# Queries' squares and query-key products as a step of their own, and eight modulation chunks in layer 0's output product instead of beside the recurrence

## The chip, the cores and the metric

The kernel runs on one core of a Trainium2 chip. The metric is the device time of one execution in microseconds (us). Five engines work side by side, each through its own queue in order: TensorE (PE, matrix products, with a separate row PEld for its weight loads), VectorE (DVE), ScalarE (ACT), GpSimd (POOL) and SyncE (SP), which only issues DMAs. Before the change the median of three runs is 1326.55 us (1324.47 to 1327.31).

## The reference

The model has two layers over 512 latent tokens of width 1024, with 256 context tokens beside them. Layer 0 mixes tokens by a bidirectional gated DeltaNet with four heads and, beside it, by pooling; layer 1 by convolutions. Each mixer is followed by a normalisation, and then by a convolutional feed-forward network (FFN) and a second normalisation. Cut to what this case touches:

```
for layer in range(2):
    mod = silu(c) @ ada_w[layer] + ada_b[layer]         # shift, scale, gate of both halves of a layer
    u = x * (1 + sc_m) + sh_m
    y = even_mixer(u, ctx_u, ...) if layer == 0 else odd_mixer(u, ...)
    x = layernorm(ALPHA * x + gt_m * y)
    y = conv_ffn(x * (1 + sc_f) + sh_f)
    x = layernorm(ALPHA * x + gt_f * y)

even_mixer:  p = u @ w_in                               # q, k, v, gate, pool, scalars
    q, k, v = silu(dwconv(p[...])); q, k = l2norm(q), l2norm(k)
    per head and chunk: a_mat = (k beta) k^T * decay;  solve (a_mat + 1);  attn = (q k^T) * decay
    recurrence over chunks, forward and backward:  v_new = u - w s;  o = q s + attn v_new;  s = s g + k v_new
    y = concat(norm(o) * silu(gate), pool(p)) @ w_out
```

The modulation vector for everything behind the first normalisation inputs is 80 columns of 128 numbers; one "chunk" below is one of these columns.

## The kernel before, in words

A product in fp32 is done as three products of split operands: a weight tile `w_raw` is rounded by ACT into `w_hi` (L167), its rest `w_lo` is formed by POOL or DVE (L173), and TensorE does `w_hi` with the high part of the activations (`ah`), `w_hi` with the low part (`al`), and `w_lo` with `ah` (the function `gemm`, L219).

Layer 0's mixer (`even`) runs a written plan, the string PLAN, one step after the other in program order. Heads are handled in two pairs, p0 and p1. In it k, q and v are the keys, queries and values of a pair (input product named `qkv_ps`, taps of a convolution on DVE, silu on ACT), e forms the systems of a pair, i and x the inverses, r the recurrence, p and w the pooling of one channel group, g a gate, d the normalised output. The system step makes decay factors (POOL forms `r` at L864, TensorE sums them into `dd_ps` at L866, ACT takes the exponential), the key-key products `kk_ps` (L885), and a small inverse whose 16x16 blocks go through a scratch buffer in memory twice (ACT issues those DMAs: L926, L930, L945, L948). The query step forms the queries; in the same step, ACT squares them (`q_sq`, L1022), TensorE sums the squares (`qn_ps`, L1025) and multiplies keys with queries (`kq_ps`, L1031), and DVE multiplies the products with the decay factors (L1034). The sums are read only by the output step, the products only by the recurrence.

Program order is not the order in which an engine works: a scheduler of the tile framework picks, for each engine, the order of its queue from the order of the program and its own estimates. On the chip each queue then runs strictly in that order.

The modulation chunks (`ada_rest`) are spread over the layer. One chunk is two DMAs of 256 KB (L360, queue of SP) and two DVE instructions of 128x512 that multiply and sum (L362), each followed by a short read of the accumulator. Before the change twelve chunks are done within step x0 (AX0 = 12) and eight within step r1 (AX1 = 8), so that twenty are done when the plan ends (`a20`). The last four before the first normalisation are done in layer 0's output product (`run`, `between`), one after each of the first four of eight output tiles (ADE = 1), from a pool of six buffers. That pool, with the tiles of the residual (`z`), comes after the mixer's pools and takes their memory.

Of the kernel before, what the change touches and what calls it, by code (L numbers as in the profile page):

```python
# [8 lines left out]
F32 = mybir.dt.float32  # L9
# [5 lines left out]
P = 128  # L15
T = 512
# [24 lines left out]
)  # L41
EVEN_SHAPES = (("tri", (4, P)), ("par", (3, P)), ("lvl", (2, P)), ("blk", (P,)), ("rev", (P,)), ("poolw", (4, P)),
               ("id16", (16,)), ("up16", (16,)), ("low16", (16,)))
PLAN = 'b0 k0 k1 e0 q0 n0 e1 q1 v0 g0 i0 n1 v1 g1 x0 p0 p1 r1 p2 g2 w2 p3 w0 g3 w3 d0 w1 d1 a20'
NI = 3
NX = 4
SHARE = 0.4
# [3 lines left out]
SHARE_DOWN = 0.5  # L51
LAST = (4, 4)
LAST_FFN = 2
ADE = 1
LATE2 = 3
READY = (2, 2)
FIRST = (3, 3, 3)
# [7 lines left out]
RINGS = ("001", "1")  # L65
RINGS_ODD = ("01", "1")
RINGS_ADA = ("01", "1")
AX0 = 12
AX1 = 8
R2 = 1  # L70
SHARE_EVEN = 0.1
# [30 lines left out]
def together(chains, n, each=None):  # L102

    active = []
    while chains or active:
        while chains and len(active) < n:
            active.append(chains.pop(0))
        for x in list(active):
            if next(x, 0) == 0:
                active.remove(x)  # L110
        if each:
            each()


class Kernel:
# [512 lines left out]
    def even(self):  # L628
        nc, a = self.nc, self.a
        with ExitStack() as ctx:  # L630
            self.rings = EVEN_RINGS
            cp = self.pool("ctx", ctx=ctx)
            km = cp.tile([P, a["even_k"].shape[1]], F32, name="even_k")
            for name, (o, shape) in EVENS.items():
                v = km[:, o:o + math.prod(shape)]
                setattr(self, name, v if len(shape) == 1 else v.rearrange("p (a b) -> p a b", b=shape[1]))
            self.ep = self.pool("even", ctx=ctx)
            self.ada_tile = lambda k: self.ep.tile([P, T], F32, tag="ada", bufs=self.bufs["ada"], name="ada_w")
            first, scal = self.start(km)
            self.ep2 = self.pool("even2", ctx=ctx)  # L640
            self.dp = ctx.enter_context(self.tc.tile_pool(name="scratch", bufs=1, space=bass.MemoryType.DRAM))
            self.gate = [None] * H
            ps, pooled, self.decays = {}, [], {}
            left = [[AX0, AX1]]

            def each(i):
                def f():
                    if left[0][i] and self.ada_next < 24:
                        left[0][i] -= 1
                        self.ada_rest(1, True)  # L650
                return f

            steps = dict(
                k=lambda p: ps.__setitem__(p, self.keys(p, None if p else first)),
                b=lambda p: self.gates(scal),
                t=lambda p: self.decays.__setitem__(p, self.decay(p)),
                n=lambda p: self.norms([ps[0], ps[1]] if p == 2 else [ps[p]]),
                e=lambda p: self.systems(p, ps[p]),
                v=lambda p: self.values(p, ps[p]),
                q=lambda p: self.queries(p, ps[p]),  # L660
                i=lambda p: together(self.inverses(p, ps[p]), NI),
                r=lambda p: together(self.recurrence(p, ps[p]), 2, each(1)),
                x=lambda p: together(self.recurrence(0, ps[0]) + self.inverses(1, ps[1]), NX, each(0)),
                y=lambda p: together(self.inverses(0, ps[0]) + self.inverses(1, ps[1]), NX),
                z=lambda p: together(self.recurrence(0, ps[0]) + self.recurrence(1, ps[1]), 4),
                a=lambda n: self.ada_rest(n - self.ada_next, True),
                g=lambda h: self.gating(h),
                p=lambda g: pooled.append(self.pooling(g)),
                w=lambda g: self.pool_out(g, pooled[g]),
                d=lambda p: together(self.gdn_out(p, ps[p]), 4),  # L670
            )
            for w in PLAN.split():
                steps[w[0]](int(w[1:]))
            for i, x in enumerate([*pooled, *self.gate]):
                self.split(x, self.ah[i], self.al[i], nc.vector if i % 2 else None)
        self.dbg("mixh", self.ah)
        self.dbg("mixl", self.al)
# [335 lines left out]
    def queries(self, p, s):  # L1013
        nc = self.nc
        qx = s["q"] = (self.lat("ql", f"p{p}"), None)
        for i in range(2):
            self.qkv(2 * p + i, qx[0][i], None)
        qs = s["qs"] = self.small("qss", [4, 2])
        pn = self.gd("qn_ps")
        for h in range(2):  # L1020
            sq = self.big("q_sq")[:, 0:T]
            nc.scalar.activation(out=sq, in_=qx[0][h], func=AF.Square)  # L1022
            for i in range(4):
                o = 2 * (2 * i + h)
                nc.tensor.matmul(out=pn[:, o:o + 2], lhsT=sq[:, i * P:(i + 1) * P], rhs=self.ones[:, 0:2], start=True,  # L1025
                                 stop=True)
        for j in (1, 2):
            ps = self.gd4("kq_ps")
            for q in range(4):
                c = 2 * j + q // 2  # L1030
                nc.tensor.matmul(out=ps[:, q], lhsT=self.chunk(s["k"], c, q % 2), rhs=self.chunk(qx, c, q % 2),  # L1031
                                 start=True, stop=True)
            e = s["e"][j]
            nc.vector.tensor_tensor(out=e, in0=ps, in1=e, op=MUL)  # L1034

        nc.vector.tensor_scalar(out=qs, in0=pn[:, 0:16].rearrange("p (c h t) -> p c h t", h=2, t=2)[:, :, :, 0],
                                scalar1=RMS_EPS * P, scalar2=RMS_EPS * RMS_EPS * P, op0=MUL, op1=ADD)
# [262 lines left out]
    def run(self):  # L1300
        nc, a = self.nc, self.a
        self.share = SHARE_EVEN
        self.late = iter(())
        self.ready = []
        self.cols = {}
        self.constants()
        self.bufs = BUFS
        pa = self.pool("a")
        self.ah = [pa.tile([P, T], F32R, name=f"ah{k}") for k in range(KD)]
        self.al = [pa.tile([P, T], F32R, name=f"al{k}") for k in range(KD)]  # L1310
        self.wp = self.pool("w")
        self.ps = self.pool("ps", psum=True)
        self.turn = {}
        self.even()
        if self.stop == "even":
            return
        self.rings = RINGS
        up = self.pool("u")
        self.uh = [up.tile([P, T], F32R, name=f"uh{k}") for k in range(KD)]
        self.ul = [up.tile([P, T], F32R, name=f"ul{k}") for k in range(KD)]  # L1320
        self.tp = self.pool("tmp")
        zp = self.pool("z")
        self.zs = [zp.tile([P, T], F32, name=f"z{k}") for k in range(KD)]
        for k in range(KD):
            nc.sync.dma_start(out=self.zs[k], in_=a["xT"][:, k])
            nc.scalar.activation(out=self.zs[k], in_=self.zs[k], func=AF.Copy, scale=ALPHA)
        self.gt_m0 = self.mods(0, 8, "mod_g")
        with ExitStack() as ctx:
            ap = self.pool("ada", ctx=ctx)
            self.ada_tile = lambda k: ap.tile([P, T], F32, tag="ada", bufs=6, name="ada_w")  # L1330
            def between(m):
                if self.ada_next < 24:
                    self.ada_rest(min(ADE, 24 - self.ada_next))
                    if self.ada_next >= 24:
                        self.columns(0)

            ring = lambda nm: ap.tile([P, T], F32R, tag="w", bufs=4 * LAST[0], name=nm)
            self.out_proj(a["even_out"], KD, self.ah, self.al, self.gt_m0, 0, self.uh, self.ul,
                          ahead=AHEAD, ring=ring, between=between,
                          first=[a["ffn_up"][0, i * KF] for i in range(READY[0])])  # L1340
        self.dbg("xm0", self.zs)
        if self.stop == "mix0":
            return

        self.ffn(0, lambda: self.gt_f0, 1)
        self.dbg("xf0", self.zs)
        if self.stop == "ffn0":
            return
        self.odd()
        self.dbg("xm1", self.zs)  # L1350
        if self.stop == "mix1":
            return
        self.ffn(1, lambda: self.gt_f1, None)
# [91 lines left out]
```

## Time and profile before

| | us |
|---|---|
| median of three runs | 1326.55 |
| lowest and highest | 1324.47, 1327.31 |
| the profiled execution's own time | 1322.59 |
| its span, first to last instruction | 1320.8 |

| engine | busy us | share of the span | instructions |
|---|---|---|---|
| PE | 1259.7 | 95% | 6690 |
| DVE | 912.2 | 69% | 1874 |
| POOL | 669.1 | 51% | 607 |
| ACT | 583.0 | 44% | 1091 |

The mean granted clock of TensorE is 0.985. These shares are means over stages: layer 0's mixer takes about the first 330 us, the output product of layer 0 runs from there to about 403 us, and behind that come FFN 0, layer 1 and FFN 1. In the FFNs TensorE is busy nearly all the time; in the mixer DVE and TensorE take turns at waiting. The busy rows show how full an engine was in a stretch; the waits, which engine and instruction it was that ended an idle time.

### The profile page before, as it was taken

How to read it: one execution, taken by the hardware profiler on the slowest of the kernel's cores; microseconds unless marked ns; L12 is line 12 of the kernel's file. 1: busy time of each engine (PE TensorE's matmuls, PEld its weight loads, DVE VectorE, ACT ScalarE, POOL GpSimd, SP SyncE). 2: the span in 40 equal slices, each digit the busy share in tenths (PEclk: the TensorE clock that was granted, in tenths of full speed). 3: DMA queues.
4: the chain of work that ended last, by engine and by line, in shares of the span. 5: the costliest groups of instructions: out<-in, count | busy, mean ns of one | idle time of the engine just before them, and what ended most of it. 6: DMA issues, size and time to landing. Idle time of an engine off the chain costs nothing.

```text
span 1320.8 us, 19563 instructions
## 1 busy us (share of the span) xinstructions
PE 1259.7 (95%) x6690; PEld 1062.0 (80%) x6690; DVE 912.2 (69%) x1874; ACT 583.0 (44%) x1091; POOL 669.1 (51%) x607
## 2 busy tenths in 40 slices
PE   6998889988899999999999999899999999999997
PEld 3877778877798888888888887688988888888886
DVE  3778899998777877788444568857786666661125
ACT  3645324356556333333322684535653333332235
POOL 2354466665426555555344667954243443433453
PEclk9998899999999999999999999999999999999998
DMA  9511213431623656556565432233032233333334
GB/s 363 194 49 39 66 45 112 145 113 32 216 88 118 193 195 196 193 192 195 171 210 155 147 95 84 69 96 128 18 112 96 96 97 100 99 92 96 95 111 135
DMA packets 100340, 166.58 MB, mean 126 GB/s; under 512 B 20432, under 2 KB 25616, under 8 KB 100240
## 3 DMA queue, kind: packets, MB, share of 16 engines
q1 hardware_dynamic: 89280, 164.09, 38.9%
q10 hardware_dynamic: 10960, 1.25, 0.7%
q8 instruction: 53, 0.87, 0.3%
q14 instruction: 47, 0.39, 0.1%
HBM read 162.60 MB, written 2.69 MB: 125 GB/s over the span
## 4 chain that ended last, share of the span: by engine, by line
PE 62%; DVE 6%; ACT 3%; POOL 2%; issue 2%; DMA 1%; POOLq 0%; ACTq 0%; SPq 0%
PE prod_ps L219 36%; PE out_ps L219 21%; PE half_ps L219 2%; DVE conf_y L1236 2%; PE ln_e L417 1%; POOL w_lo L173 1%; POOL conf_far L1225 1%; DVE z L478 1%; PE ln_w L427 1%; DVE w_lo L173 1%; ACT w_hi L167 1%; DVE ln_d L424 1%; ACT ln_u L490 0%; DMA w_raw<-in_even_out 0%; DVE ln_s L404 0%
## 5 line engine op out<-in xcount | busy, mean ns | idle before, releaser
L173 POOL TENSOR_TENSOR w_lo<-w_raw,w_hi 128x512 fp32r<-128x512 f32 (+1 forms) x302 | 392.8, 1304 | 456.4 <-ACT w_hi L167 441.0
L167 ACT CAST w_hi<-w_raw 128x512 fp32r<-128x512 f32 (+1 forms) x408 | 245.7, 608 | 457.0 <-PE prod_ps L219 140.2
L219 PE MATMUL prod_ps<-uh,w_lo 128*128 128x512 f32 x792 | 309.8, 391 | 5.0 <-POOL w_lo L173 3.7
L219 PE MATMUL prod_ps<-uh,w_hi 128*128 128x512 f32 x792 | 309.3, 391 | 2.7 <-ACT w_hi L167 2.7
L219 PE MATMUL prod_ps<-ul,w_hi 128*128 128x512 f32 x792 | 309.2, 390 | 0.0
L604 DVE SCALAR_TENSOR_TENSOR f_acc<-prod_ps,prm,f_acc 128x441 f32<-128x441 f32 (+2 forms) x320 | 222.2, 694 | 61.4 <-ACT f_acc L593 52.1
L219 PEld LDWEIGHTS prod_ps<-uh,w_lo 128*128 128x128 f32 x792 | 149.4, 189 | 37.8 <-POOL w_lo L173 5.0
L219 PEld LDWEIGHTS prod_ps<-uh,w_hi 128*128 128x128 f32 x792 | 149.3, 189 | 33.7 <-ACT w_hi L167 3.1
L219 PEld LDWEIGHTS prod_ps<-ul,w_hi 128*128 128x128 f32 x792 | 149.3, 188 | 31.0
L173 DVE TENSOR_TENSOR w_lo<-w_raw,w_hi 128x512 fp32r<-128x512 f32 (+1 forms) x106 | 85.0, 802 | 123.5 <-ACT w_hi L167 121.6
L219 PE MATMUL out_ps<-ah,w_lo 128*128 128x256 f32 (+1 forms) x352 | 118.1, 335 | 3.8 <-DVE w_lo L173 3.8
L219 PE MATMUL out_ps<-ah,w_hi 128*128 128x256 f32 (+1 forms) x352 | 118.1, 336 | 1.6 <-ACT ah L456 1.6
L219 PE MATMUL out_ps<-al,w_hi 128*128 128x256 f32 (+1 forms) x352 | 118.7, 337 | 0.0
L219 PE MATMUL out_ps<-hh,w_lo 128*128 128x512 f32 (+1 forms) x280 | 99.2, 354 | 1.9 <-POOL w_lo L173 1.9
L219 PE MATMUL out_ps<-hh,w_hi 128*128 128x512 f32 (+1 forms) x280 | 98.7, 352 | 0.1
L219 PE MATMUL out_ps<-hl,w_hi 128*128 128x512 f32 (+1 forms) x280 | 98.6, 352 | 0.0
L362 DVE SCALAR_TENSOR_TENSOR ada_w<-ada_w,crow_ps 128x512 f32<-128x512 f32 x112 | 70.7, 682 | 10.1 <-DMA ada_w<-in_ada 10.1
L219 PEld LDWEIGHTS out_ps<-ah,w_lo 128*128 128x128 f32 x352 | 67.0, 190 | 10.8 <-DVE w_lo L173 4.1
L219 PEld LDWEIGHTS out_ps<-ah,w_hi 128*128 128x128 f32 x352 | 67.0, 191 | 8.7 <-ACT ah L456 2.0
L219 PEld LDWEIGHTS out_ps<-al,w_hi 128*128 128x128 f32 x352 | 67.2, 191 | 7.5 <-DVE al L457 0.8
L219 PEld LDWEIGHTS out_ps<-hh,w_lo 128*128 128x128 f32 x280 | 53.4, 191 | 9.7 <-POOL w_lo L173 2.1
L219 PEld LDWEIGHTS out_ps<-hh,w_hi 128*128 128x128 f32 x280 | 53.4, 191 | 7.9 <-ACT w_hi L167 0.3
(362 smaller groups left out, 2285.9 us busy)
## 6 DMA issues: line engine op xcount, KB each, us to landing
w_raw<-in_ffn_up SPq DMA_DIRECT2D x176, 256.0 KB, 2.6
ada_w<-in_ada SPq DMA_DIRECT2D x160, 256.0 KB, 3.7
w_raw<-in_ffn_down SPq DMA_DIRECT2D x100, 256.0 KB, 2.8
w_raw<-in_even_in SPq DMA_DIRECT2D x40, 256.0 KB, 2.8
w_raw<-in_odd_in SPq DMA_DIRECT2D x40, 256.0 KB, 2.9
ada_w<-in_ada SPq DMA_DIRECT2D x16, 512.0 KB, 8.4
w_raw<-in_even_out SPq DMA_DIRECT2D x16, 256.0 KB, 2.9
w_raw<-in_odd_out SPq DMA_DIRECT2D x16, 256.0 KB, 2.7
```

The costliest lines, as they stand in the source:

```text
L167: r = nc.scalar.copy(out=hi[:, :n], in_=raw)
L173: r = eng.tensor_tensor(out=lo[:, :n], in0=raw, in1=hi[:, :n].bitcast(F32), op=SUB)
L219: r = nc.tensor.matmul(out=o, lhsT=w, rhs=x[k][:, c0:c1], start=clear and k == i == 0, stop=k == n - 1 and i == 2, skip_group_check=pin)
L362: r = nc.vector.scalar_tensor_tensor(out=w, in0=w, scalar=1.0, in1=c, op0=MUL, op1=MUL, accum_out=self.mod[:, k, i:i + 1])
L417: nc.tensor.matmul(out=pe[:, 2 * (n * e + i):2 * (n * e + i) + 2], lhsT=t[:, i * P:(i + 1) * P], rhs=ones, start=e == 0 and i == 0 and not ...
L424: nc.vector.tensor_tensor(out=d[:, 0:n], in0=self.ident[:, None, :].broadcast_to([P, n, P]), in1=x.broadcast_to([P, n, P]), op=MUL)
L427: nc.tensor.matmul(out=o, lhsT=self.ones, rhs=d[:, 0:n].rearrange("p a b -> p (a b)"), start=True, stop=True)
L478: nc.vector.tensor_tensor(out=z, in0=z, in1=x, op=op)
L604: nc.vector.scalar_tensor_tensor(out=o, in0=sv[:, r0 + dr:r1 + dr, q0 + dc:q1 + dc], scalar=w[:, tap:tap + 1], in1=o, op0=MUL, op1=ADD)
L1225: nc.gpsimd.tensor_tensor(out=far, in0=far, in1=f, op=ADD)
L1236: nc.vector.scalar_tensor_tensor(out=o, in0=pa[:, max(0, d):T - max(0, -d)], scalar=w[:, tap:tap + 1], in1=o, op0=MUL, op1=ADD)
```

## The change

The query step is cut in two. Forming the queries stays where it was (q0, q1 in the plan); the squares, their sums and the key-query products become the step u, which stands in the plan behind the values of the same pair: u0 behind v0, u1 behind v1. Step x0 does eight modulation chunks and no longer twelve, sixteen are done when the plan ends, and layer 0's output product does two after each of the first four output tiles, eight in all, from a pool of eight buffers.

```diff
-PLAN = 'b0 k0 k1 e0 q0 n0 e1 q1 v0 g0 i0 n1 v1 g1 x0 p0 p1 r1 p2 g2 w2 p3 w0 g3 w3 d0 w1 d1 a20'
+PLAN = 'b0 k0 k1 e0 q0 n0 e1 q1 v0 u0 g0 i0 n1 v1 u1 g1 x0 p0 p1 r1 p2 g2 w2 p3 w0 g3 w3 d0 w1 d1 a16'
-ADE = 1
+ADE = 2
-AX0 = 12
+AX0 = 8
                 q=lambda p: self.queries(p, ps[p]),
+                u=lambda p: self.attention(p, ps[p]),
...
         for i in range(2):
             self.qkv(2 * p + i, qx[0][i], None)
+
+    def attention(self, p, s):
+
+        nc = self.nc
+        qx = s["q"]
         qs = s["qs"] = self.small("qss", [4, 2])
         pn = self.gd("qn_ps")
         for h in range(2):
...
-            self.ada_tile = lambda k: ap.tile([P, T], F32, tag="ada", bufs=6, name="ada_w")
+            self.ada_tile = lambda k: ap.tile([P, T], F32, tag="ada", bufs=8, name="ada_w")
             def between(m):
                 if self.ada_next < 24:
                     self.ada_rest(min(ADE, 24 - self.ada_next))
```

From the new method on, lines are six further down in the changed kernel (L1025 is L1031 there); between L659 and there they are one further down.

On TensorE, where the squares of the first pair are summed before (`qn_ps`), right behind the first of the queries' input products, and ahead of the second pair's decay sums (`dd_ps`) and key-key products (`kk_ps`):

```order
L219 MATMUL qkv_ps<-ah_74,w_hi 128x512
L219 MATMUL qkv_ps<-al_82,w_hi 128x512
L219 MATMUL qkv_ps<-ah_74,w_lo 128x512
L1025 MATMUL qn_ps<-ones,q_sq 128x2 x4
L1031 MATMUL kq_ps<-ql,kl 128x128 x3
L1025 MATMUL qn_ps<-ones,q_sq 128x2 x4
L1031 MATMUL kq_ps<-ql,kl 128x128 x5
L866 MATMUL dd_ps<-r,even_k 128x256 x12
L885 MATMUL kk_ps<-kc 128x128 x4
L885 MATMUL kk_ps<-kl 128x128 x8
```

The same sums and products in the changed kernel, 118 places further on, with input products on both sides:

```order
L219 MATMUL qkv_ps<-ch,w_lo 128x256
L219 MATMUL qkv_ps<-ch,w_hi 128x256
L219 MATMUL qkv_ps<-cl,w_hi 128x256
L1031 MATMUL qn_ps<-ones,q_sq 128x2 x4
L1037 MATMUL kq_ps<-ql,kl 128x128 x2
L1031 MATMUL qn_ps<-ones,q_sq 128x2 x4
L1037 MATMUL kq_ps<-ql,kl 128x128 x6
L992 MATMUL it_ps<-r_1507,kk 128x128 x2
```

The sums now stand in front of the first product of the inverses (`it_ps`). The second pair's decay sums have moved the other way: in the changed kernel they stand only twelve input products (the last three are shown) behind the first pair's key-key products, where 77 stood between before.

```order
L886 MATMUL kk_ps<-kc 128x128 x4
L886 MATMUL kk_ps<-kl 128x128 x8
L219 MATMUL qkv_ps<-al_89,w_hi 128x512
...
L219 MATMUL qkv_ps<-al_84,w_hi 128x512
L219 MATMUL qkv_ps<-ah_76,w_lo 128x512
L219 MATMUL qkv_ps<-ah_77,w_hi 128x512
L867 MATMUL dd_ps<-r,even_k 128x256 x12
L886 MATMUL kk_ps<-kc 128x128 x4
L886 MATMUL kk_ps<-kl 128x128 x8
```

On DVE, from the last low parts of the mixer's output (`al_89`) through the modulation chunks (`ada_w`) to the first `w_lo` of the output product, before:

```order
L457 TENSOR_TENSOR al_89<-gate,ah_81 128x512
L362 SCALAR_TENSOR_TENSOR ada_w,mod<-ada_w,crow 128x512
L524 SCALAR_TENSOR_TENSOR z_3479<-out_ps,mod_g,z_3479 128x512
L362 SCALAR_TENSOR_TENSOR ada_w,mod<-ada_w,crow 128x512 x3
L524 SCALAR_TENSOR_TENSOR z_3480<-out_ps,mod_g,z_3480 128x512
L362 SCALAR_TENSOR_TENSOR ada_w,mod<-ada_w,crow 128x512
...
L404 TENSOR_TENSOR ln_s_3622<-ln_s_3622,ln_sq 128x512
L362 SCALAR_TENSOR_TENSOR ada_w,mod<-ada_w,crow 128x512 x2
L173 TENSOR_TENSOR w_lo<-w_raw,w_hi 128x512
```

The end of the same stretch in the changed kernel, where nine further chunk instructions stand ahead of the rows shown:

```order
L362 SCALAR_TENSOR_TENSOR ada_w,mod<-ada_w,crow 128x512 x5
L524 SCALAR_TENSOR_TENSOR z_3458<-out_ps,mod_g,z_3458 128x512
L362 SCALAR_TENSOR_TENSOR ada_w,mod<-ada_w,crow 128x512
L401 TENSOR_TENSOR ln_s_3597<-ln_s_3597,z_3458 128x512
L404 TENSOR_TENSOR ln_s_3598<-ln_s_3598,ln_sq 128x512
L362 SCALAR_TENSOR_TENSOR ada_w,mod<-ada_w,crow 128x512
L173 TENSOR_TENSOR w_lo<-w_raw,w_hi 128x512
```

Between `al_89` and the first `w_lo` there were 8 chunk instructions, 3 of `z` and 4 of the normalisation's sums; now there are 16, 4 and 6. On SP the 16 chunk loads stand in one run ahead of the eight loads of `even_out`, where 8 stood before.

## Rows read from the trace of the kernel before

**Rows 1.** By stage: start:end, length, busy us (instructions) of each engine, clock, DMA, GB/s.

```profile
92.50:112.00 19.50, 15.56 (x82) 12.88 (x80) 17.39 (x33) 9.07 (x14) 15.68 (x22) 1.00 0.22 52
112.00:145.00 33.00, 33.00 (x173) 29.32 (x173) 29.52 (x77) 14.80 (x20) 12.13 (x13) 0.90 0.16 47
145.00:165.00 20.00, 15.96 (x89) 14.56 (x88) 16.41 (x35) 7.82 (x14) 8.64 (x10) 0.83 0.31 59
190.00:290.00 100.00, 93.04 (x635) 80.56 (x636) 93.27 (x252) 42.54 (x122) 68.71 (x80) 1.00 0.34 109
345.00:368.00 23.00, 18.86 (x122) 17.50 (x121) 21.05 (x39) 9.71 (x18) 8.66 (x6) 0.93 0.57 180
```

The engines stand in the order PE, PEld, DVE, ACT, POOL.

**Rows 2.** PE's waits, 40 to 420 us: who waited for whom, total us, times, longest.

```profile
PE qn_ps L1025 <- ACT q_sq L1022: 6.7, 2, 3.5
PE out_ps L219 <- DVE w_lo L173: 3.8, 1, 3.8
PE it_ps L991 <- DVE r L984: 3.7, 7, 1.0
```

**Rows 3.** ACT in time, at both stalls: start, duration, what, [idle before <- releaser].

```profile
105.29 0.41 ACTq L926 DMA_DIRECT2D scr<-cb  x1
...
109.06 0.35 ACTq L930 DMA_DIRECT2D a<-scr  x1
...
146.86 0.34 ACTq L930 DMA_DIRECT2D a<-scr  x1
```

**Rows 4.** PE in time, decay and key-key products of the first pair.

```profile
84.45 5.51 PE L866 MATMUL dd_ps<-r,even_k 128*128 128x256 f32 x22
...
90.69 1.95 PE L885 MATMUL kk_ps<-kl 128*128 128x128 f32 x16
```

**Rows 5.** POOL in time, decay factors of the second pair.

```profile
97.32 6.22 POOL L864 TENSOR_TENSOR r<-even_k,sc_g 128x256 f32<-128x256 f32 x10
```

**Rows 6.** DVE groups, 205 to 300 us: count, busy us, mean ns, idle before.

```profile
L362 DVE SCALAR_TENSOR_TENSOR ada_w<-ada_w,crow 128x512 f32<-128x512 f32 x40 | 36.4, 946 | 0.2 <-issue 0.2
```

**Rows 7.** PE in time, the last recurrence products and the gate products behind them.

```profile
317.11 0.61 PE L1112 MATMUL o_ps<-vn,at 128*128 128x128 f32 x4
...
320.10 0.39 PE L219 MATMUL gate_ps<-ah,w_lo 128*128 128x512 f32 x1
320.32 0.39 PE L219 MATMUL gate_ps<-ah,w_hi 128*128 128x512 f32 x1
```

**Rows 8.** POOL in time, the last two of four additions of pooling group 3.

```profile
312.30 2.42 POOL L1172 TENSOR_TENSOR pool_q<-pool_q 128x521 f32<-128x521 f32 x2
```

**Rows 9.** DVE in time, 324 to 353 us, end of mixer and chunks.

```profile
324.52 3.19 DVE L1151 SCALAR_TENSOR_TENSOR gate<-ot_ps,prm,gate 128x128 f32<-128x128 f32 x12
...
330.88 1.41 DVE L457 TENSOR_TENSOR al<-pool_o,ah 128x512 fp32r<-128x512 f32 x1
332.21 3.48 DVE L457 TENSOR_TENSOR al<-gate,ah 128x512 fp32r<-128x512 f32 x2
341.55 0.69 DVE L362 SCALAR_TENSOR_TENSOR ada_w<-ada_w,crow 128x512 f32<-128x512 f32 x1 [5.86 <-DMA ada_w<-in_ada]
...
344.89 0.68 DVE L362 SCALAR_TENSOR_TENSOR ada_w<-ada_w,crow 128x512 f32<-128x512 f32 x1
...
345.50 0.74 DVE L524 SCALAR_TENSOR_TENSOR z<-out_ps,mod_g,z 128x512 f32<-128x512 f32 x1
346.17 0.68 DVE L362 SCALAR_TENSOR_TENSOR ada_w<-ada_w,crow 128x512 f32<-128x512 f32 x1
...
351.18 1.74 DVE L362 SCALAR_TENSOR_TENSOR ada_w<-ada_w,crow 128x512 f32<-128x512 f32 x1
...
352.86 1.74 DVE L173 TENSOR_TENSOR w_lo<-w_raw,w_hi 128x512 fp32r<-128x512 f32 x1
```

**Rows 10.** SP in time, loads of chunks and of the output weights.

```profile
335.75 8.55 SPq L360 DMA_DIRECT2D ada_w<-in_ada  x8
344.40 12.40 SPq L159 DMA_DIRECT2D w_raw<-in_even_out  x8
```

## The prediction

> **What bounds the kernel now.** I read the stages first, then who waited for whom, then the instructions in time around the longest waits. In layer 0's mixer neither engine is full: from 92.5 to 165 us DVE idles 2.1, 3.5 and 3.6 us in three stretches, 9.2 us in all, and TensorE 3.9, 0 and 4.0 us [rows 1]. The reader is to see in the same rows that the clock is below full there, 0.90 over 33 us and 0.83 over 20 us: 3.3 and 3.4 us of TensorE's time are lost to running at the lower of its two levels (1.2 instead of 2.4 GHz) after it stood still. The longest wait of TensorE up to 420 us is for the queries' squares: 6.7 us in two waits [rows 2]. ACT makes the squares, and its queue is held ahead of them by the scratch round trip: the write is issued at 105.29, the read that must wait for it only at 109.06, 3.8 us later, and the second pair's read at 146.86 stands ahead of the squares in the same way [rows 3]. From 190 to 290 us both are close to full, DVE 93.3 and TensorE 93.0 of 100 us [rows 1]; behind that, the output product has one wait of 3.8 us, for `w_lo` from DVE [rows 2], since DVE works off the chunks first [rows 9]. FFN 0 and what follows get the same work and are taken as unchanged.
>
> **Part one, the squares further on.** Both waits for squares go, since in the changed order only the products at the inverses stand behind them. TensorE gets back 6.7 us of waits and 6.7 us of clock [rows 1, 2]. It can't all show: DVE has the taps, the systems and the small inverse in the same stretch, and only its 9.2 us of idleness can be taken away [rows 1]. That is the upper end. What is late next is the second pair's decay factors. TensorE now reaches their sums twelve input products (0.23 us each [rows 7]) after the first pair's key-key products, which end at 92.6 [rows 4]: 95.4 us. POOL begins the factors at 97.3 and takes 0.62 us for each [rows 5], so twelve are there at 104.8; the sums themselves take 0.25 us each, 24 of them 6.0 [rows 4]. TensorE loses some 104.8 - 95.4 - 6.0 = 3.4 us there, and for that time fills no bank that DVE could empty. 9.2 - 3.4 leaves 5.8: I take -6. The ends are -9.2 (the new wait hidden under the first pair's system on DVE) and 0 (the new wait takes back all). The DMAs of the scratch stay on ACT's queue, with two fewer things behind them that TensorE waits for. The four activations and 32 small products are only moved.
>
> **Part two, eight chunk instructions fewer beside the recurrence.** They cost 0.95 us each there [rows 6], 7.6 us of DVE. TensorE's idleness in the hundred microseconds is 7.0 us [rows 1], which is the upper end of what can come of it; the lower is 0, if the recurrence's own chain is what TensorE waits for. The nearest row is TensorE's waits for DVE at the inverses, 3.7 us in seven [rows 2]; part of those have other causes, and I take -3. Their eight loads leave SP's queue there, and nothing waits for them (0.2 us of idleness before forty of them) [rows 6].
>
> **Part three, the end of the mixer.** The changed order has 15 products of the last pooling group and 24 of a gate behind the last recurrence products, where 18 of a gate stood. So the pooling chain closes the mixer: 15 x 0.23 = 3.4, a copy 0.7 (taken like a DVE instruction of its size), four POOL additions 2 x 2.42 = 4.8 [rows 8], DVE's difference and edges 1.6 (between 0.7 and 1.7 for a tile [rows 9], and something for the edges), sixteen gate multiplications at 3.19/12 = 4.3, four splits 0.7 + 1.4 + 3.5 = 5.6 [rows 9]: 20.4 us. Before, from the end of the last recurrence products at 317.7 to the last split's end at 335.7 it was 18.0 us [rows 7, 9]. That is 2.4 later; against it 21 products (4.8 us) no longer stand ahead, in a place where the recurrence may or may not use them. I take +2; the ends are -2.4 (all 4.8 are used) and +7 (the gates wait for the pooling one by one, twice over).
>
> **Part four, the output product.** Here the cost is plainest. The chunk loads can start only when the mixer's memory comes free, that is after the last split: issue at 335.75 [rows 10], first chunk instruction at 341.55 after 5.86 us of waiting, and then all chunk instructions stand ahead of the first `w_lo` at 352.86 [rows 9], which TensorE waits for. Eight more chunk instructions at a pitch of 0.61 (345.50 - 344.89) make 4.9; one `z` at 0.67 and two sums at 0.61 that now stand ahead too make 1.9; the last chunk instruction, 1.74 long, is not again that long: -1.0 [rows 9]. That is +5.8, rounded to +6. TensorE has no cover left, since it stands already. The lower end is 3.9 (the `z` and sums would have been in the way later anyway), the upper 11 x 0.75 = 8.3, 0.75 being the mean of this stretch (11.3 us for fifteen). The loads do not set it: sixteen at 8.55/8 = 1.07 us are issued by 352.9, eight buffers being enough for the eight instructions done by then, and the output weights behind them [rows 10] land before or about when DVE is through, near 358.8. The lower clock behind the wait (0.93 over 23 us, 1.6 us lost [rows 1]) is there now and stays.
>
> What the row shows of the price by place: 0.95 us from 190 to 290 us, where POOL is busy 69 of 100 us, and 0.61 at 345 [rows 1, 6, 9]. The Trainium skill (SBUF — State Buffer, section Who interferes with whom) says that a VectorE instruction with two inputs from SBUF and a GpSimd instruction that reads SBUF shut each other out for a whole instruction. The trace agrees. By the rule the eight give up 7.6 us and cost 4.9; without it they would cost 7.6 in the new place too, and the sum would be 2.7 higher.
>
> **Sum.** -6 - 3 + 2 + 6 = -1 us. Against the profiled execution's 1322.59 that is 1321.6; that execution lies 4.0 below the median of 1326.55, and to the median the same sum gives 1325.5.
>
> **Rivals.** First: the stalls' time is won nearly whole, and the recurrence uses DVE's free time. For it: both engines idle at the same time in 145 to 165, and the waits are long and few; against it: DVE was 89% full from 112 to 145 [rows 1]. With all upper ends of parts one and two and no late pooling it gives -9.2 - 7.0 + 6 = -10; halfway between that and my sum, -5.5: 1321.
>
> Second, on the other side: the late pooling chain decides. The loads of all sixteen chunks start only after the last split, so every microsecond by which the pooling of the last group is late is paid in full by `w_lo`. For it: POOL's additions and splits run up to twice as long where DVE reads two tiles; against it: 24 gate products cover part. At its end of +7 the sum is -6 - 3 + 7 + 6 = +4: 1330.5. It decides from +5.7 on, where the whole is slower by 0.2%.
>
> Third, also slower: the decay factors take the stalls' place. TensorE stands still for POOL at 95 us, and its clock falls as it did after the waits for squares, 3.3 us [rows 1]; DVE, with no products to take, loses all that part one gives: 0 - 3 + 2 + 6 = +5: 1331.5. For it: POOL works one factor per 0.62 us and sums need 0.5 [rows 4, 5]; against it: DVE has the first pair's system to do meanwhile. The Trainium skill (TensorE: Matmul & The Clock Gate, section HAM oscillation — how this bites in real kernels) says that idle gaps of TensorE between bursts bring the low clock back each time. The trace agrees where waits were 3.2 to 3.8 us long; whether this wait is long enough no run here shows.
>
> **How the numbers follow.** A change of 0.2%, 2.65 us, is about what a measurement of this kernel can tell from none. My forecast gets 0.43, with its own range 1321 to 1330: of this 0.13 faster, 0.25 within, 0.05 slower. The first rival has 0.27, all faster. The second has 0.15: 0.12 slower, 0.03 within. The third has 0.15: 0.12 slower, 0.03 within. Together faster 0.40, same 0.31, slower 0.29. The range goes from the first rival's far end, -10 and so 1317, to the third with the upper price of part four, +7.3, and so 1334.
>
> **What would show it.** Right: no wait of TensorE for `q_sq`, clock near 1.00 from 112 to 165; decay sums that wait for POOL at about 95 to 105; the first product of the inverses some 6 us earlier; sixteen chunk instructions in one row behind the last split, and a wait of `out_ps` for `w_lo` near 10 us. Wrong: chunk instructions there that do not delay `w_lo` (the cost of part four would be gone), or a last split that ends later than 335.7 (parts one and two would be gone). The stretch from the first normalisation on should be as long as before, to a microsecond.

## The result and the profile after

The changed kernel is slower. Its median is 1334.36 us (1329.23 to 1336.58, six runs) beside 1324.12 us (1320.39 to 1327.31, six runs) for the kernel before; the ratio is 1.0073, with a 95% interval from 1.0058 to 1.0088. Its profiled execution took 1333.64 us with a span of 1331.9, 11.1 us more than the span before.

Busy time by stage of the changed kernel, the stretches and columns of [rows 1]:

```profile
92.50:112.00 19.50, 16.94 (x81) 13.25 (x81) 16.12 (x35) 8.41 (x11) 16.09 (x25) 0.91 0.12 25
112.00:145.00 33.00, 28.18 (x141) 23.53 (x140) 32.25 (x87) 12.38 (x20) 12.00 (x12) 0.95 0.28 72
145.00:165.00 20.00, 18.68 (x121) 15.76 (x120) 19.96 (x42) 5.04 (x9) 10.00 (x11) 1.00 0.22 58
190.00:290.00 100.00, 92.70 (x640) 80.37 (x639) 85.16 (x227) 42.23 (x126) 63.47 (x75) 1.00 0.32 101
345.00:368.00 23.00, 12.63 (x56) 10.63 (x55) 20.96 (x48) 5.93 (x10) 4.80 (x4) 0.75 0.55 176
```

From 112 to 165 us DVE idles 0.8 us where it idled 7.1, and the clock is 0.95 and 1.00 where it was 0.90 and 0.83: the stalls for the squares are gone. TensorE did not stand still for less time, though: in the first three stretches it idles 8.7 us in all, where it idled 8.0 [rows 1]. From 190 to 290 us DVE is 8.1 us less busy and TensorE is not busier. In the output product TensorE stands still for 10.4 of 23 us, where it was 4.1.

TensorE's waits in the changed kernel, 40 to 430 us, columns as in [rows 2]:

```profile
PE pool_y L1193 <- DVE pool_o L1187: 6.7, 1, 6.7
PE out_ps L219 <- ACT w_hi L167: 5.2, 1, 5.2
PE out_ps L219 <- DVE w_lo L173: 5.2, 1, 5.2
PE dd_ps L867 <- POOL r L865: 2.6, 1, 2.6
PE qkv_ps L219 <- DVE ql L810: 2.4, 1, 2.4
PE v_ps L833 <- ACT vc L812: 2.3, 1, 2.3
...
PE qn_ps L1031 <- ACT q_sq L1028: 0.6, 1, 0.6
```

The 6.7 us for the squares have become 0.6, but waits of 2.6 us for the decay factors, 2.4 for the queries (`ql`) and 2.3 for the values (`vc`), all between 92.5 and 145 us, have come in their place. Three waits are longer than any single one of before (3.8 us, for `w_lo`): 6.7 us for the last pooling group and 5.2 us twice in the output product.

Three places divide the span: the end of the last recurrence products, the issue of the first chunk load of the output product (the mixer's memory is free), and the first whole product of FFN 0. Up to the first of them, the changed kernel and then the kernel before, columns as above:

```profile
92.50:309.20 216.70, 199.02 (x1287) 171.20 (x1287) 192.47 (x507) 86.94 (x214) 127.08 (x153) 0.98 0.25 71
92.50:317.70 225.20, 204.98 (x1303) 178.13 (x1302) 205.54 (x523) 95.09 (x222) 138.74 (x159) 0.97 0.27 80
```

The three stretches against before, in us, with the two experiments that do one part of the change each:

| kernel | last recurrence products end at | from there to the first chunk load | from there to FFN 0 | FFN 0 and all behind it | span |
|---|---|---|---|---|---|
| before | 317.7 | 18.1 | 67.4 | 917.6 | 1320.8 |
| changed | 309.2 | 28.3 | 75.6 | 918.8 | 1331.9 |
| new step alone | 317.2 | 19.0 | 70.7 | 915.1 | 1322.0 |
| chunks alone | 319.3 | 27.8 | 74.8 | 920.9 | 1342.8 |

So of the 11.1 us the recurrence gives -8.5, the end of the mixer +10.2, the output product +8.2, and the rest +1.2. The rest differs by up to 5.8 us among these four executions, so that +1.2 says nothing.

The end of the mixer, TensorE, then POOL, then DVE of the changed kernel in order of time (start, duration, what, idle before and releaser):

```profile
318.59 0.39 PE L219 MATMUL gate_ps<-ah,w_lo 128*128 128x512 f32 x1
325.69 2.08 PE L1193 MATMUL pool_y<-pool_o,even_k 128*128 128x512 f32 x2 [6.71 <-DVE pool_o L1187]
```

```profile
314.00 1.46 POOL L173 TENSOR_TENSOR w_lo<-w_raw,w_hi 128x512 fp32r<-128x512 f32 x1 [2.28 <-ACT w_hi L167]
315.42 1.25 POOL L1178 TENSOR_TENSOR pool_q<-pool_b 128x527 f32<-128x527 f32 x1
316.75 2.20 POOL L1178 TENSOR_TENSOR pool_q<-pool_q 128x525 f32<-128x525 f32 x2
318.91 1.29 POOL L457 TENSOR_TENSOR al<-pool_o,ah 128x512 fp32r<-128x512 f32 x1
320.13 1.29 POOL L1178 TENSOR_TENSOR pool_q<-pool_q 128x513 f32<-128x513 f32 x1
...
322.57 2.96 POOL L173 TENSOR_TENSOR w_lo<-w_raw,w_hi 128x512 fp32r<-128x512 f32 x2
332.56 4.89 POOL L457 TENSOR_TENSOR al<-gate,ah 128x512 fp32r<-128x512 f32 x2 [7.02 <-ACT ah L456]
```

```profile
321.45 1.74 DVE L1182 SCALAR_TENSOR_TENSOR pool_o<-pool_q,pool_b 128x512 f32<-128x512 f32 x1 [5.71 <-POOL pool_q L1178]
323.22 1.19 DVE L1186 TENSOR_TENSOR pool_o<-pool_q,prm 128x8 f32<-128x8 f32 x2
324.37 1.27 DVE L1187 TENSOR_TENSOR pool_o<-pool_o,pool_b 128x8 f32<-128x8 f32 x2
328.23 3.87 DVE L1157 SCALAR_TENSOR_TENSOR gate<-ot_ps,prm,gate 128x128 f32<-128x128 f32 x14 [2.60 <-PE ot_ps L1152]
```

TensorE has done its last gate product at 319 and stands until the pooled group is there. POOL has put a `w_lo` ahead of the four additions and a split among them; DVE's difference takes 1.74 us and its edge instructions of eight columns 0.6 each, beside a `w_lo` on POOL. The gate multiplications, though they need nothing of the pooling, are behind it in DVE's queue and behind `pool_y` through TensorE's. The last splits are POOL's and end at 337.4, when the first chunk load is issued.

The output product, DVE and SP of the changed kernel, answering to [rows 9, 10]:

```profile
342.59 1.81 DVE L362 SCALAR_TENSOR_TENSOR ada_w<-ada_w,crow 128x512 f32<-128x512 f32 x1 [7.57 <-DMA ada_w<-in_ada]
...
360.65 1.75 DVE L362 SCALAR_TENSOR_TENSOR ada_w<-ada_w,crow 128x512 f32<-128x512 f32 x1
...
362.33 1.73 DVE L173 TENSOR_TENSOR w_lo<-w_raw,w_hi 128x512 fp32r<-128x512 f32 x1
```

```profile
337.47 15.59 SPq L360 DMA_DIRECT2D ada_w<-in_ada  x16
353.16 13.12 SPq L159 DMA_DIRECT2D w_raw<-in_even_out  x8
```

From the first chunk instruction to the first `w_lo` it is 19.7 us, where it was 11.3 [rows 9]. The output weights' loads begin 15.7 us after the first chunk load's issue (353.16 - 337.47), where it was 8.7 [rows 10].

### The profile page after: what moved, and what is told of

Read it like the earlier page. It is cut to its first block, busy times and chain, and to the rows that moved or that the text cites. A ratio compares the mean times of both kernels' runs of the same rounds, so it can differ in the third digit from the quotient of the medians.

```text
span 1331.9 us, 19543 instructions
## 1 busy us (share of the span) xinstructions
PE 1262.4 (95%) x6690; PEld 1062.3 (80%) x6690; DVE 904.8 (68%) x1874; ACT 577.4 (43%) x1087; POOL 667.9 (50%) x607
## 4 chain that ended last, share of the span: by engine, by line
PE 62%; DVE 8%; POOL 3%; ACT 3%; issue 2%; DMA 1%; POOLq 0%; ACTq 0%; SPq 0%; DVEq 0%
PE prod_ps L219 36%; PE out_ps L219 20%; PE half_ps L219 2%; DVE conf_y L1242 2%; DVE ada_w L362 1%; DVE z L478 1%; PE ln_e L417 1%; POOL w_lo L173 1%; POOL conf_far L1231 1%; DMA ada_w<-in_ada 1%; DVE w_lo L173 1%; PE ln_w L427 1%; ACT w_hi L167 1%; DVE ln_d L424 1%; DVE z L524 0%
## 5 line engine op out<-in xcount | busy, mean ns | idle before, releaser
L219 PE MATMUL prod_ps<-uh,w_hi 128*128 128x512 f32 x792 | 309.2, 390 | 2.7 <-ACT w_hi L167 2.7
L362 DVE SCALAR_TENSOR_TENSOR ada_w<-ada_w,crow_ps 128x512 f32<-128x512 f32 x112 | 70.7, 682 | 9.0 <-DMA ada_w<-in_ada 8.9
```

Of the source, the lines that this page charges most:

```text
L219: r = nc.tensor.matmul(out=o, lhsT=w, rhs=x[k][:, c0:c1], start=clear and k == i == 0, stop=k == n - 1 and i == 2, skip_group_check=pin)
L362: r = nc.vector.scalar_tensor_tensor(out=w, in0=w, scalar=1.0, in1=c, op0=MUL, op1=MUL, accum_out=self.mod[:, k, i:i + 1])
```

## The experiments

Theory A: each part of the change does what its place in the queues says; the loss is the late pooling chain plus the chunk instructions in front of the first `w_lo`. Its rivals are named with each kernel. Times of one kernel scatter by 5 to 12 us from run to run, so stretches of the profiled executions carry the finer points.

**The new step alone.** The changed kernel with the chunks put back:

```diff
-... r1 p2 g2 w2 p3 w0 g3 w3 d0 w1 d1 a16'
+... r1 p2 g2 w2 p3 w0 g3 w3 d0 w1 d1 a20'
-ADE = 2
+ADE = 1
-AX0 = 8
+AX0 = 12
-tag="ada", bufs=8
+tag="ada", bufs=6
```

> The new step for squares and key-query products alone; chunks as before (twelve beside the recurrence, four in the output product, six buffers). Theory A (the gain of part one is real, the loss comes whole from the chunks): the first product of the inverses some 7 us earlier than before (about 155 instead of 162 us), the pooling of the last group again finished ahead of the last recurrence products, the wait for w_lo again 3.8 us; total 6 to 8 us faster than before (1316 to 1318). Rival B (the new step itself makes the end of the mixer late, since all engines' orders change): wait of the pooling product near 6.7 us here too, total within 3 us of before. Rival C (the gain of part one is lost again in the recurrence whatever the chunks do): total within 3 us of before with no wait for pooling.

Measured: 1324.57 us beside 1323.74 before, ratio 1.0005 (0.9990 to 1.0019): no change, as rival C had it. The first product of the inverses comes at 155.4 instead of 161.9 us, the last one at 273.1 instead of 272.8, and the last recurrence products end at 317.2 instead of 317.7. The 6.5 us were not a gain. TensorE up to that first product and from there to the end of the last one, before and then with the new step alone:

```profile
92.50:161.90 69.40, 61.41 (x324) 54.11 (x323) 60.21 (x137) 30.83 (x44) 35.20 (x42) 0.90 0.23 54
161.90:273.10 111.20, 104.16 (x707) 89.82 (x706) 103.84 (x266) 37.65 (x104) 72.07 (x86) 1.00 0.29 90
```

```profile
92.50:155.40 62.90, 55.45 (x297) 46.34 (x296) 57.68 (x143) 24.72 (x38) 35.18 (x44) 0.95 0.23 60
155.40:273.40 118.00, 111.58 (x739) 96.63 (x738) 102.07 (x262) 38.41 (x106) 72.29 (x85) 0.97 0.27 85
```

TensorE is 6.0 us less busy in the first stretch and 7.4 us busier in the second. In part that is work put behind the milestone: ten input products and the second pair's sums and key-query products stood ahead of it before and stand behind it now. In part it is the clock, which is better in the first stretch (0.95 for 0.90) and worse in the second (0.97 for 1.00, some 3.5 us). There is no wait for the pooling (1.0 us) and none for `w_lo`; but the output product took 3.3 us longer all the same. TensorE's wait there, and the clock behind it:

```profile
PE ln_e L417 <- DVE ln_s L401: 3.3, 1, 3.3
```

```profile
365.00:380.00 15.00, 12.86 (x67) 12.63 (x68) 7.51 (x22) 3.64 (x7) 0.61 (x1) 0.66 0.17 51
```

Having lost the wait for `w_lo`, TensorE runs into the normalisation's sums, 3.3 us, and then works at the lower level: 5.1 us lost in these 15 us, where the kernel before lost 1.6 behind its wait [rows 1].

**The chunks alone.** The kernel before with AX0 = 8, ADE = 2, eight buffers and `a16` (the reverse of the diff above).

> The move of eight chunk instructions alone; queries' step as before. Theory A: both losses are here (late pooling, some 9 us from the last recurrence product to the last split, and 8 to 10 us in the output product), less some 1.7 us won beside the recurrence: 15 to 17 us slower than before (1339 to 1341). Rival B (the late pooling belongs to the new step): only the output product's 8 to 10 us less what is won beside the recurrence: 6 to 8 us slower (1330 to 1332), no wait for pooling.

Measured: 1340.09 beside 1323.74 us, ratio 1.0127 (1.0107 to 1.0147): 16 us slower, as theory A said (its profiled execution, in the table, is the slowest of its five runs, 1344.68). The wait for the squares is there as before (6.3 us). Its next waits on TensorE, 40 to 430 us:

```profile
PE pool_y L1187 <- DVE pool_o L1181: 5.9, 1, 5.9
PE out_ps L219 <- DVE w_lo L173: 5.5, 1, 5.5
PE out_ps L219 <- ACT w_hi L167: 4.5, 1, 4.5
```

The late pooling and both waits of the output product come with the chunks and not with the new step. In TensorE's order 13 products of the last pooling group stand behind the last recurrence products here, 15 in the changed kernel, none with the new step alone: fewer chunks beside the recurrence make the scheduler bring the recurrence forward past the pooling. The two parts do not add up, though: 16 and 1 us apart, 10 together. With the new step the recurrence ends 10.1 us earlier than with the chunks alone, where it ends 1.6 us later than before (table).

**One chunk per tile, and `w_lo` on POOL.** Two edits of the changed kernel:

```diff
-ADE = 2
+ADE = 1
```

> The changed kernel with one chunk after each of eight output pieces instead of two after each of four: eight chunk instructions stand ahead of the first w_lo, as before the change, and eight behind it. Theory A (what costs in the output product is what stands in the queues ahead of the first w_lo, DVE's and SP's): the two waits of TensorE there (5.2 and 5.2 us) shrink to one near 4 us, first w_lo about 8 us after the position it had relative to the first chunk instruction, total 5 to 8 us faster than the changed kernel (1326 to 1329). Rival D (sixteen chunk instructions cost what they cost, wherever in the stage): the rest of the waits appears behind w_lo, total within 2 us of the changed kernel.

```diff
-SHARE_OUT = (0.5, 0.5)
+SHARE_OUT = (0, 0.5)
```

> The changed kernel with all w_lo of the output product's last four tiles formed by GpSimd, none by DVE, so that no w_lo stands behind chunk instructions. Theory A: the wait for w_lo (5.2 us) goes, the wait for w_hi (5.2 us, output weights loaded behind sixteen chunk loads) stays, GpSimd's 1.3 us for each of eight w_lo are mostly hidden: 3 to 5 us faster than the changed kernel (1329 to 1331). Rival E (the loads alone set the output product): no gain, within 1.5 us of the changed kernel, TensorE waiting for w_hi or for the landing instead.

Measured: 1331.35 (ratio to before 1.0058, 1.0039 to 1.0077) and 1339.01 us (1.0117, 1.0097 to 1.0136). The first is between what the two theories expected, and its interval overlaps the changed kernel's; its output product takes 75.4 us, so rival D holds for the stretch. The second is slower than the changed kernel, which nobody expected: the output product takes 78.0. The waits of the one and of the other in this stretch:

```profile
PE out_ps L219 <- DVE w_lo L173: 4.2, 4, 2.1
PE ln_e L417 <- DVE ln_s L401: 3.4, 1, 3.4
```

```profile
PE ln_e L417 <- DVE ln_s L404: 3.6, 1, 3.6
PE out_ps L219 <- ACT w_hi L167: 3.4, 1, 3.4
```

In both the wait for `w_lo` shrinks (to 1.2 us, for POOL's, in the second) and a wait for the sums takes its place.

**Loads and instructions of the chunks apart.** In the changed kernel's output product, for every second chunk, once the loads are left out and the instructions run on the chunk before, and once the instructions are left out and the loads stay (a constant in place of these modulation columns). The mixer's order is untouched by either.

```diff
+                if 16 <= i < 24 and i % 2:
+                    w = self.held[k]
+                else:
...
```

> The changed kernel with the loads of every second chunk in the output product left out (their instructions run on the chunk before, so this part of the modulation is not the reference's): 16 chunk instructions, 8 loads. The order of the mixer is the changed kernel's. Theory F (DVE's queue alone sets the first w_lo; the late loads of the output weights only show ahead of it): the wait for w_hi (5.2 us) is gone or under 1 us, the wait for w_lo is 8 to 11 us, from the first chunk load's issue to FFN 0's first whole product 74 to 76 us as in the changed kernel (75.6), total within 2 us of it. Rival G (the loads alone set it): that stretch near before's 67.4 us, total 6 to 8 us faster than the changed kernel.

```diff
+                if 16 <= i < 24 and i % 2:
+                    continue
                 c = self.crow_ps[k] if self.crow_ps else self.crow[:, cs]
```

> The changed kernel with DVE's instructions of every second chunk in the output product left out, their loads kept (this part of the modulation is a constant and not the reference's): 8 chunk instructions, 16 loads. The order of the mixer is the changed kernel's. Theory F: the wait for w_lo (5.2 us) goes, that for w_hi (4 to 5.5 us) stays, because the output weights are still loaded behind sixteen chunk loads: from the first chunk load's issue to FFN 0's first whole product 70 to 72 us, total 1328 to 1331. Rival G (the loads alone set it): that stretch 74 to 76 us, no gain. Rival H (DVE alone): 67 to 68 us, 1325 to 1327.

Measured: 1334.04 and 1330.21 us beside 1323.65 (ratios 1.0080, 1.0067 to 1.0092, and 1.0047, 1.0034 to 1.0060). Theory F is met in both, but for the wait for `w_hi` in the second, which was to stay at 4 to 5.5 us. The waits of the one and of the other:

```profile
PE out_ps L220 <- DVE w_lo L174: 9.9, 1, 9.9
```

```profile
PE out_ps L220 <- ACT w_hi L168: 2.7, 1, 2.7
```

Without the loads the two waits of 5.2 us become one of 9.9, and from the first chunk load's issue (338.1) to FFN 0 (413.4) it is 75.3 us: DVE's sixteen instructions alone make the whole cost. Without the instructions it is 70.3 us (338.9 to 409.2): the loads alone still cost 3, as the output weights come late. The costs lie beside each other and do not add.

**The last pooling group earlier, and chunks in r1.** The changed kernel with p3 ahead of g2; then with four of the moved chunks in r1 besides; then with seven.

```diff
-... p1 r1 p2 g2 w2 p3 w0 g3 w3 d0 w1 d1 a16'
+... p1 r1 p2 p3 g2 w2 w0 g3 w3 d0 w1 d1 a16'
```

> The changed kernel with the last pooling group's product ahead of the gate of head 2 in the plan, so that no pooling product stands behind the last recurrence products and 28 gate products do. Theory A (the late pooling chain is what takes back the gain at the mixer's end): the 6.7 us wait of the pooling product goes, the first chunk load is issued 4 to 7 us earlier than at 337.5, total 1328 to 1331 (the changed kernel is at 1334.4). Rival C (the end of the mixer is set by the work of TensorE and DVE as a whole; what is not waited for at the end was done in front of it): the last recurrence products come 4 us or more later than at 309, the first chunk load within 2 us of 337.5, total within 2 us of the changed kernel.

```diff
+... p1 r1 p2 p3 g2 w2 w0 g3 w3 d0 w1 d1 a20'
-ADE = 2
+ADE = 1
-AX1 = 8
+AX1 = 12
```

> The changed kernel with the last pooling group ahead of the gate of head 2, and four of the eight moved chunks in step r1 (twelve there rather than eight), so that the output product has four again, one after each tile: a candidate for a better version. Theory A: DVE idles in a third of the stretch 290 to 330 of the changed kernel, so the four chunks cost little there; output product near 67.4 to 70.6 us as in the kernels with four chunks, the first chunk load between 332 and 337: total 1322 to 1328. Rival C: the four chunks cost DVE 6 to 8 us at the end of the mixer as well, first chunk load after 339, total 1328 to 1332.

The same with AX1 = 15 and `a23`:

> As the kernel with four chunks more in step r1 and the last pooling group ahead of the gate of head 2, but fifteen chunks in r1, so that a single one (two instructions) is left in the output product. Theory A (the chunk instructions in front of the first w_lo are the cost, DVE in r1 has room): wait for w_lo under 1 us, output product 63 to 67 us from the last split, first chunk load before 340: total 1318 to 1323. Rival C (DVE's work as a whole sets the mixer's end): each of three more chunks costs 1.5 us there, first chunk load after 340, total 1322 to 1327. Rival I (with the wait for w_lo gone TensorE runs into the sums of the normalisation instead, and its clock falls there): a wait of ln_e near 3 us and output product near 70 us, total 1323 to 1327.

Measured: 1331.69 (ratio 1.0055, 1.0036 to 1.0074), 1322.98 (0.9987, 0.9973 to 1.0000) and 1324.05 us (1.0005, 0.9988 to 1.0022), each beside its own runs of before (1323.65, 1323.65 and 1323.15). In the first the wait for the pooling is gone, the first chunk load is issued at 333.2 instead of 337.5, and the last recurrence products start at 312.7 instead of 308.9: both theories are half right. Of the 4.3 us, 3.8 are lost again in the output product, 79.4 us long. Its waits:

```profile
PE out_ps L219 <- ACT w_hi L167: 5.3, 1, 5.3
PE out_ps L219 <- DVE w_lo L173: 4.2, 1, 4.2
PE ln_e L417 <- DVE ln_s L401: 2.7, 1, 2.7
```

The second is back at the time of before, as theory A had it, with a wait for `w_lo` of 3.2 us, an output product of 66.7 us and the first chunk load at 336.8. The third has no wait for `w_lo` (output product 63.7 us), and its first chunk load comes at 338.1, both as theory A had them: its profiled span is 1319.0, but its twelve runs do not tell it from before, and their median lies where rival C put it. No version beats the kernel before clearly.

**p3 ahead of r1**, once with a single chunk in the output product (ADE = 1, AX1 = 15 as above) and once with four. In both the last two pooling groups get each other's weights and places, so that their output is not the reference's; the work is the same.

```diff
-... x0 p0 p1 r1 p2 g2 w2 p3 w0 g3 w3 d0 w1 d1 a16'
+... x0 p0 p1 p3 r1 p2 g2 w2 w0 g3 w3 d0 w1 d1 a23'
```

> The same single chunk in the output product, with the last pooling group ahead of step r1. Theory A: no gate or pooling product is left behind the last recurrence products, so that TensorE goes over into the output product at once; first chunk load before 338, total 1316 to 1323. Rival C: the last recurrence products come past 320 us, since the products that stood behind them now stand in front, and the end of the mixer is no earlier than before's 335.8: total 1322 to 1328.

With `a20`, AX1 = 12:

> The changed kernel with four of the moved chunks in r1 (four stay in the output product) and the last pooling group ahead of step r1, eight gate products behind the last recurrence products. Theory A: first chunk load between 331 and 336, output product near 67 us, total 1318 to 1323. Rival C: no earlier than 335.8, total 1322 to 1327.

Measured: 1324.66 (ratio 1.0008, 0.9994 to 1.0022) and 1328.03 us (1.0032, 1.0016 to 1.0049). Rival C holds, but for the second total, 1 us above its range: the last recurrence products start at 327.2 and 324.8 us, the first chunk load is issued at 343.1 and 340.2. With more products in front of them, the recurrence ends later.

**The new step alone, with the sums on POOL.**

```diff
-                    self.ln_partial(zs[m], st, *half, False, nc.vector if nk == KD else None)
+                    self.ln_partial(zs[m], st, *half, False, nc.vector if nk == KD and odd else None)
```

> The kernel with the new step alone (chunks as before), with the normalisation's sums of the output product's last four tiles on GpSimd and no longer on DVE. In that kernel TensorE waited 3.3 us for the sums (ln_e for ln_s) and ran below full clock from 365 to 380 us, 5 us lost. Theory I (the wait for w_lo, gone there, came back as this wait): with the sums out of DVE's queue the wait shrinks under 1.5 us and the clock stays near 1.00 from 365 to 380, output product 65 to 67 us instead of 70.6, total 1319 to 1321. Rival: GpSimd is slower at the sums and the wait grows past 4 us, total 1325 to 1329.

Measured: 1324.50 us (ratio 1.0011, 0.9997 to 1.0025). The rival holds for the wait, and the total lies just below its range; theory I's 65 to 67 us for the output product are missed (72.6). TensorE's wait:

```profile
PE ln_e L417 <- POOL ln_s L401: 4.3, 1, 4.3
```

From 365 to 380 us the clock is 0.66 here too.

## Why the prediction was wrong, point by point

The direction and the size were wrong: a sum of -1 us was forecast, and the spans differ by +11.1.

- **Part one and part two** stood as -6 and -3 up to the last recurrence products; -8.5 was measured there. The number is met, but that is luck: each part alone moved this point by -0.5 and +1.6 us (table), and only the two together by -8.5. It was also read as time won. TensorE was 6.0 us less busy up to it (199.0 us, 205.0 before): the stages of [rows 1] have 3.4 us at the lower clock where they had 6.7, and the 21 products now behind this point are some 4.8 us by the prediction's 0.23 each; the runs do not part the two further. The 9.2 us of idle DVE were real, and DVE was given the next instructions; TensorE was not given less to do. The new step alone shows it best: +6.5 us of lead at 155 us, none at 273. The decay sums waited 2.6 us for POOL and then took 7.8 us for 24, not 6.0: 4.4 us lost where 3.4 were worked out. The waits of 2.4 and 2.3 us for `ql` and `vc` were not in the sum.
- **Part three is the step that failed**: +2 with ends -2.4 and +7, against +10.2. The chain was worked out at 20.4 us; it took 28.3. By links, the forecast in brackets: products 3.4 (3.4), to the first addition 2.8 (0.7, ACT and POOL each did another weight tile first), additions 6.0 (4.8, a split among them), difference and edges 4.2 (1.6), `pool_y` and transposes 2.6 (left out), gate multiplications 4.3 (4.3), splits 4.9 (5.6, all of them DVE's; the last to end were two of POOL's, beside four on DVE), to the load's issue nothing. A chain's own instructions were added up, and what stands between them in each queue was not. The credit of 4.8 us for the products moved was not seen at all in the place where it was looked for: it can only be in the 6.0 us above. The second rival named this mechanism and had 0.15; its price of +7 was too low by 3. (It has POOL's additions and splits up to twice as long beside DVE; in the trace before the longest addition is 1.54 us, the shortest 1.06.) The prediction's own sign of being wrong came: the last split ended at 337.4 us, later than 335.7.
- **Part four** was +6 with an upper end of 8.3, and +8.2 was measured; the chunk instructions were to cost 0.61 each and most did, but the first two took 1.8 us each and the last 1.75 again. That the wait would be near 10 us was right: 5.2 for `w_hi` and 5.2 for `w_lo`, and 9.9 in one with the loads left out. That the loads do not set it holds only beside the instructions: alone they cost 3 us. The lower clock was to cost the same as before. Its share is larger now (0.75 over 23 us, 0.93 before), but TensorE stood still for much of that time: from the end of its last wait to FFN 0 it took 49.0 us (364.1 to 413.1), where it took 48.6 (354.6 to 403.2).
- **The third rival** did not decide: the wait for the decay factors did lower the clock, to 0.66 from 100 to 105 us, but the sums took no longer for it (last section), DVE went on with the first pair's system, and the first product of the inverses came at 155.0 us, 6.9 earlier than before.

What stays open is why the scheduler, with fewer chunks beside the recurrence, puts the pooling behind it; that the two go together is shown by the two kernels with one part each.

The Trainium skill (SBUF — State Buffer, section Who interferes with whom) says that a VectorE instruction with two inputs from SBUF and a reading GpSimd instruction exclude each other whole. The trace agrees at the pooling's edges: two multiplications of 128x8 took 1.19 us and two subtractions 1.27, beside two `w_lo` on POOL from 322.6 to 325.5; in the trace before the same pairs took 0.43 and 0.23 us. The prediction had 1.6 us for the difference and the edges together.

## What to carry to other kernels

A milestone that comes earlier is a gain only if as much was done before it: compare the busy time up to it, not its time alone. A chain that closes a stage is priced by the queues it passes through, with what else stands in each, and a second engine's chain (here the gates) may be tied behind it by order alone. Work moved into the shadow of a wait moves the end of that wait where the awaited instruction stands behind it in the same queue, here almost one to one (8.4 us more from the first chunk instruction to the first `w_lo`, a stage 8.2 us longer), and when such a wait is taken away the next dependency, here the normalisation's sums, may take the same time back.

## What the runs showed of the hardware

A wait of 2.6 us of TensorE was followed by the lower clock. The decay sums of the second pair in the changed kernel, and the stretch of 5 us in which most of them ran:

```profile
98.79 7.81 PE L867 MATMUL dd_ps<-r,even_k 128*128 128x256 f32 x24 [2.56 <-POOL r L865]
```

```profile
100.00:105.00 5.00, 5.00 (x16) 3.85 (x16) 4.93 (x14) 3.07 (x4) 5.00 (x8) 0.66 0.02 3
```

24 of them took 7.81 us, where 22 took 5.51 [rows 4]. The clock is not the reason. In the kernel with one chunk per tile, whose mixer has the same order, the same wait was not followed by the lower clock, and the sums took as long:

```profile
99.18 7.81 PE L867 MATMUL dd_ps<-r,even_k 128*128 128x256 f32 x24 [2.58 <-POOL r L865]
```

```profile
100.00:105.00 5.00, 4.93 (x17) 2.37 (x17) 4.93 (x14) 3.22 (x4) 5.00 (x9) 1.00 0.01 3
```

What paced them in both is POOL, which makes one factor for every two of these matmuls and took 7.7 us for its twelve in either kernel; in the changed one:

```profile
98.13 7.72 POOL L865 TENSOR_TENSOR r<-even_k,sc_g 128x256 f32<-128x256 f32 x12
```

Twelve kernels here have this wait of 2.6 us. In nine of them the clock fell behind it, in three (one chunk per tile, and both with p3 ahead of r1) it did not, and in all twelve the sums took 7.8 us. So the length of a wait did not decide alone whether the clock fell, and the lower clock cost nothing where another engine set the pace. Where TensorE had work that it could do at once, it did cost: behind the 3.3 us of waiting for the sums, the kernel with the new step alone lost 5.1 us more.
